# A decoder trunk on one core: the residual stream scaled once, and the MLP's operand blocks formed in a fixed order

## The chip, the cores and the metric

The kernel runs on 1 core of one Trainium2 chip. The metric is the device time of one execution in microseconds (us); lower is better. A core has TensorE (PE in the profile, with its weight loads as PEld), VectorE (DVE), ScalarE (ACT), GpSimd (POOL) and SyncE (SP), whose queue issues the DMA transfers.

## The reference, cut to what matters

One layer over 1024 tokens of width 1024: three parallel mixers behind one projection, a cross-attention to 256 memory tokens, and an MLP with a squared ReLU. The change lies in the last two sub-layers:

```
def rms_norm(x, g):
    y = x32 * lax.rsqrt(jnp.mean(x32 * x32, axis=-1, keepdims=True) + EPS)
    return y * g

h += CrossAttn(RMSNorm(h), RMSNorm(mem))        # 4 heads of 256, QK-norm, 256 memory tokens
h += W_down( relu(RMSNorm(h) @ W_up)^2 )        # 1024 -> 4096 -> 1024
```

Everything is float32. A per-token factor can be moved past a matrix product over channels, and past the squared ReLU as its square.

## The kernel before

The stream h is held transposed, channels on partitions: eight tiles `ht[0]` to `ht[7]` of 128 x 1024 (all tokens). A float32 product is made of three faster ones: each operand is split into a rounded high half (a cast on ScalarE) and the low half that remains (a subtraction on VectorE or POOL), and high x high, high x low and low x high are summed in PSUM.

*Order.* The program is traced once; a scheduler then puts each engine's instructions in order by priority and by the times that it expects, with a higher priority for what stands under `tc.high_priority()`. PE's instructions are bound: from early on each goes through `tc.keep_in_program_order`, which puts it behind the instruction of its engine that was traced just before. VectorE, ScalarE, POOL and SP are not bound here. Small side jobs wait in a list; `step()` in the loops of matmuls takes at most one due job from it, `after(n, fn)` adds one that is due n steps later, `drain()` empties it. A pool gives out tiles by tag; a tile waits until a slot of its tag is free.

*Cross-attention.* `queries(h)` projects the queries of a head (with `rx`, the tokens' RMS factor from `factors`, due after 2 steps), `attend` queues the scores, the softmax (`rd` is the reciprocal of its sum), the turns and the values. The output projection is made in two parts: `parts0` (heads 0 and 1) for all eight tiles, then `parts1` (heads 2 and 3); `project` adds each PSUM result to `ht[i]` (L1319). PSUM has two wide tiles (`pg`, 1024 columns) and four single banks (`pss`, 512 columns).

*Start of the MLP.* The second part, `parts1`, is interleaved with the forming of the MLP's operands. For a couple of tiles i = kp and kp + 4, kp = 0 to 3: `project`; store `ht[i]` to DRAM (`d_h`); form `v` = ht x gain x rbx (L1391), where `rbx` is `rx` spread over 128 partitions (a VectorE product to `hx_dg`, PE products with a matrix of ones, two ScalarE copies) at the start of this stage. The up-projection is a fast 2 x 2 block product with seven products instead of eight (Strassen's, in Winograd's form): on the token side `v` gives four halves x11, x12, x21, x22 of 512 columns, and the differences t1 to t4. Seven of these are split per couple by `slice_of` (cast L1358, subtraction L1359) into tiles `blk` that stay for the whole up-projection.

```
                dve.tensor_sub(t2, b22, t1)
                slice_of("t2", t2)
                ...
                dve.tensor_sub(t2, b21, t2)
                slice_of("t4", t2)
```

*Up-projection.* 16 pairs of weight tiles; class `Pair` loads them, forms the sums of the weight side on VectorE (`sums`, L1459 to L1463, and L1470), splits seven stationary blocks per pair (`stationary`: cast L1421, subtraction on POOL L1422) and makes seven products of 12 matmuls (`product`). The first group of products is (0,1), (0,5), (1,1), (1,5), written as (pair, product), then 6, 2, 3, 7, 4 of pair 0 and of pair 1; each later pair goes through 6, 1, 5, 7, 2, 3, 4. `result` sums the products: `p1` is a copy of product 1 (L1495), `u2` adds product 6 (L1498), `u5` adds product 5 (L1501); then come the squared ReLU and a store to `d_r`. The temporary t2 (which becomes t4) and `u2` share one tile, t3 and `u5` another, t1 and `p1` two.

*Down-projection.* Two halves of four output tiles q = 0 to 3; q < 2 lie in the wide PSUM tiles, q >= 2 in single banks. Over 32 operands, each loaded from `d_r` (`r_in`) and split (L1074, L1075) in blocks of four, runs `product(k, q, h)`: three matmuls, h being the half of the tokens. The last block goes output by output, and each half result is multiplied by the factor `f[0]` (L1589), added to the stream (`hv`, loaded from `d_h`; L1590) and stored. `f[0]` is (r / rx)^2, where r is the RMS factor of the stream before the MLP; `factor` makes it during the up-projection from the squares of the stored `d_h`.

Of the kernel before, what the change touches and what calls it, by code (L numbers as in the profile page):

```python
# [17 lines left out]
P = 128  # L18
D = 1024
# [36 lines left out]
def trunk_kernel(tc, w_io):  # L56
# [3 lines left out]
    with ctx:  # L60
# [76 lines left out]
        d_z = dram.tile([16, P, T], F32, name="d_z")  # L137
        d_cs = dram.tile([8, 32, P], F32, name="d_cs")
        d_h = dram.tile([8, P, T], F32, name="d_h")
        d_r = dram.tile([32, P, T], F32, name="d_r")  # L140
# [107 lines left out]

        def token_rstd(pool_, acc, n, scale, eps, name):
# [5 lines left out]
            return rsqrt_small(pool_, st[:, :nt], nt, scale, eps, name)  # L255

# [951 lines left out]
        with ExitStack() as sc:  # L1208
# [4 lines left out]
            def factors():  # L1213
# [3 lines left out]
                dve.tensor_mul(rx2[0], rx[0], rx[0])  # L1217

            after(2, factors)
            xg = qp.tile([P, 2], F32, name="xg")  # L1220
            dve.tensor_scalar(xg, C("xq_g", 0, 2), 1.0 / 16, None, ALU.mult)
# [32 lines left out]
            def attend(h, qT, outs, start):  # L1254
# [10 lines left out]
                def scores(t2):  # L1265
# [14 lines left out]
                    for j in range(2):  # L1280
# [32 lines left out]

            def project(parts, slot, i2, j):
# [4 lines left out]
                dve.tensor_add(hv, hv, ps)  # L1319

# [33 lines left out]

        def slice_of(name, src):
            pool_, tag = next(spares)
            t = pool_.tile([P, 2, 512], F32R, tag=tag, name="blk")
            act.copy(t[:, 0, :], src)  # L1358
            dve.tensor_sub(t[:, 1, :], src, t[:, 0, :].bitcast(F32))  # L1359
            blocks.setdefault(name, []).append(t)  # L1360

        f = []

        def factor():

            r = token_rstd(xr, sums[0], T, 1.0 / D, EPS, "hm")
            q = xr.tile([P, NT], F32, name="rq")
            dve.reciprocal(q, rx[0])
            dve.tensor_mul(q, q, r)
            dve.tensor_mul(q, q, q)  # L1370
            rb = xr.tile([P, T], F32, tag="acc", name="rb")
            dg = opa.tile([P, T], F32, tag="ol", name="f_dg")
            f.append(rb)
            after(4, lambda: spread(xr, q, T, "f", rb, dg))

        with ExitStack() as sc:
            mp = sc.enter_context(tc.tile_pool(name="up", bufs=1))

            rbx = opd.tile([P, T], F32, tag="sl", name="rbx")
            dg = opd.tile([P, T], F32, tag="sl", name="hx_dg")  # L1380
            after(0, lambda: spread(xr, rx[0], T, "hx", rbx, dg))
            for kp in range(4):
                if kp % 2 == 0:
                    slots = [wslot(w_io["w_xo"][1, kp // 2 + 2 * q]) for q in range(2)]
                vs = []
                for q in range(2):
                    i = kp + 4 * q
                    project(parts1, slots[q], i // 2, kp % 2)
                    nc.sync.dma_start(d_h[i], ht[i])
                    v = opd.tile([P, T], F32, tag="sl", name="v")  # L1390
                    dve.scalar_tensor_tensor(v, ht[i], C("g_mlp", i), rbx, ALU.mult, ALU.mult)  # L1391
                    vs.append(v)
                    lo_, hi_ = v[:, :512], v[:, 512:]
                    if q == 0:
                        slice_of("x11", lo_)
                        t1 = mp.tile([P, 512], F32, tag="p1", name="t1", bufs=2)
                        dve.tensor_sub(t1, hi_, lo_)
                        slice_of("t1", t1)
                t2 = mp.tile([P, 512], F32, tag="u2", name="t2")
                t3 = mp.tile([P, 512], F32, tag="u5", name="t3")  # L1400
                b12, (b21, b22) = vs[0][:, 512:], (vs[1][:, :512], vs[1][:, 512:])
                dve.tensor_sub(t2, b22, t1)
                slice_of("t2", t2)
                slice_of("x21", b21)
                slice_of("x22", b22)
                dve.tensor_sub(t3, b22, b12)
                slice_of("t3", t3)
                dve.tensor_sub(t2, b21, t2)
                slice_of("t4", t2)

            nstat = [0]

            def stationary(src):
# [8 lines left out]
                pool.tensor_sub(t[:, 1, :], src, t[:, 0, :].bitcast(F32))  # L1422
                return t
# [16 lines left out]
            class Pair:  # L1440
# [9 lines left out]

                def sums(self, n):

                    if n not in self.s:
                        a11, a12, a21, a22 = self.a
                        if n == 2:
                            self.sums(1)
                        self.s[n] = t = mp.tile([P, 512], F32, tag="s", name="s", bufs=3)
                        if n == 1:
                            dve.tensor_add(t, a21, a22)  # L1459
                        elif n == 2:  # L1460
                            dve.tensor_sub(t, self.s[1], a11)  # L1461
                        else:
                            dve.tensor_sub(t, a11, a21)  # L1463
                    return self.s[n]

                def weights(self, j):
                    a11, a12, a21, a22 = self.a
                    if j == 3:
                        s2 = self.sums(2)
                        dve.tensor_sub(s2, a12, s2)  # L1470
                        src = s2
                    elif j in (1, 2, 4):
                        src = {1: a11, 2: a12, 4: a22}[j]
                    else:
                        src = self.sums({5: 1, 6: 2, 7: 3}[j])
                    self.st[j] = stationary(src)

# [36 lines left out]


            ORDER = (6, 1, 5, 7, 2, 3, 4)
            groups = [[(0, 1), (0, 5), (1, 1), (1, 5)] + [(pr, j) for pr in range(2) for j in (6, 2, 3, 7, 4)]]
            groups += [[(pr, j) for j in ORDER] for pr in range(2, 16)]
            for group in groups:
                pairs = {}  # L1520
                with tc.high_priority():
                    for pr, j in group:
                        if pr not in pairs:
                            pairs[pr] = Pair(pr)
                        pairs[pr].weights(j)
                for pr, j in group:
                    if j == ORDER[0] and 2 <= pr < 10:
# [6 lines left out]
        if True:  # L1534
            for hf in range(2):
                outs = []
                for q in range(4):
                    if q < 2:
                        ps = pg.tile([P, T], F32, tag="g", name="ps_d")
                        outs.append([ps[:, :512], ps[:, 512:]])  # L1540
                    else:
                        outs.append([pss.tile([P, 512], F32, tag="s", name="ps_d2") for h in range(2)])
                hs = []
                for blk in range(8):
# [36 lines left out]
                    for q in range(4):  # L1581
                        i = hf * 4 + q
                        o = hp.tile([P, T], F32, tag=f"ht{i}", name="o")
                        for h in range(2):
                            sl = slice(h * 512, h * 512 + 512)
                            for k in range(4):
                                product(k, q, h)
                            step()
                            dve.tensor_mul(o[:, sl], outs[q][h], f[0][:, sl])  # L1589
                            dve.tensor_add(o[:, sl], o[:, sl], hs[q][:, sl])  # L1590
                            nc.sync.dma_start(w_io["outT"][i][:, sl], o[:, sl])

# [106 lines left out]
```

## Time and profile before

| what | value |
|---|---|
| three runs | 2753.6, 2754.24, 2755.34 us; median 2754.24 |
| the profiled execution | 2757.7 us, its span 2755.9 us |
| PE busy | 2701.6 us, 98% of the span |
| VectorE busy | 1635.2 us, 59% |
| ScalarE busy | 1054.2 us, 38% |
| POOL busy | 883.9 us, 32% |
| mean granted TensorE clock | 0.992 |

The span runs from the first to the last instruction. Rows of the timeline give start, duration, engine, line, operation, output <- inputs, shapes and count; in brackets stands how long the engine was idle before, and what released it. A row with "x9" merges nine instructions. Rows of waits give the engine that waited, for which engine and line, the sum in us, how often, and the longest. Rows of groups give count, busy us, mean ns, and idle time before.

### The profile page before, as it was taken

The page shows a single profiled execution, that of the slowest core. Times are in us where ns is not written, and L with a number is a line of the kernel's source. Part 1 is how long each engine was busy: PE and PEld are TensorE (multiplying, and loading weights), DVE is VectorE, ACT ScalarE, POOL GpSimd, SP SyncE. Part 2 cuts the span into 40 slices and gives each one's busy share as a digit, 9 for nine tenths or more (in the row PEclk, how much of TensorE's full clock was granted, in tenths as well). Part 3 has the DMA queues.
Part 4 walks back from the last instruction along what each step waited for, and adds up shares of the span by engine and source line. Part 5 has one row for each costly group of instructions (what it writes and reads, how often), then busy time and mean ns, then how long its engine had stood idle before and what let it go on. Part 6 is the DMA issues. An engine that isn't in the chain of part 4 may idle for free. (4 is left out here: it accounts for less than half of the span.)

```text
span 2755.9 us, 32424 instructions
## 1 busy us (share of the span) xinstructions
PE 2701.6 (98%) x12720; PEld 2183.4 (79%) x12720; DVE 1635.2 (59%) x1883; ACT 1054.2 (38%) x1780; POOL 883.9 (32%) x442
## 2 busy tenths in 40 slices
PE   9999999999999999999899999999998999999999
PEld 7888878887787878765588878899776888888787
DVE  7588878758777876634314774323367886522423
ACT  6523321123555555556511351236433322232221
POOL 2322211202625253424242432321115664322120
PEclk9999999999999999999999999999999999999999
DMA  7542232321333232442444333311123332554541
GB/s 251 196 130 99 100 107 94 107 99 39 119 119 119 96 126 104 165 149 75 135 174 160 108 107 99 100 54 39 47 84 107 145 130 107 186 181 145 191 131 68
DMA packets 113386, 330.19 MB, mean 120 GB/s; under 512 B 11329, under 2 KB 36433, under 8 KB 112849
## 3 DMA queue, kind: packets, MB, share of 16 engines
q1 hardware_dynamic: 113232, 328.12, 35.0%
q8 instruction: 100, 1.64, 0.2%
q14 instruction: 54, 0.43, 0.0%
HBM read 252.42 MB, written 78.80 MB: 120 GB/s over the span
## 5 line engine op out<-in xcount | busy, mean ns | idle before, releaser
L160 POOL TENSOR_TENSOR wl<-ws,wh 128x1024 fp32r<-128x1024 f32 (+1 forms) x153 | 383.6, 2509 | 1058.3 <-ACT wh L159 996.2
L336 DVE SCALAR_TENSOR_TENSOR tapy<-hin,cst,tapy 128x1024 f32<-128x1024 f32 x240 | 387.6, 1615 | 31.8 <-ACT tapy L331 25.5
L159 ACT CAST wh<-ws 128x1024 fp32r<-128x1024 f32 (+1 forms) x169 | 176.3, 1044 | 450.1 <-PE ps_g L73 271.4
L73 PE MATMUL ps_g<-uh,wh 128*128 128x512 f32 x1008 | 330.1, 406 | 2.0 <-ACT uh L369 1.5
L73 PE MATMUL ps_g<-ul,wh 128*128 128x512 f32 x1008 | 323.7, 396 | 0.5 <-DVE ul L370 0.5
L73 PE MATMUL ps_up<-blk,st 128*128 128x512 f32 x1344 | 311.3, 394 | 8.9 <-DVE blk L1359 5.7
L73 PE MATMUL ps_g<-uh,wl 128*128 128x512 f32 x1008 | 315.6, 392 | 1.5 <-POOL wl L160 1.5
L73 PEld LDWEIGHTS ps_up<-blk,st 128*128 128x128 f32 x1344 | 255.3, 190 | 64.2 <-DVE blk L1359 6.3
L73 PE MATMUL ps_g<-oh,wh 128*128 128x512 f32 x768 | 245.7, 401 | 6.6 <-ACT oh L1074 4.0
L73 PE MATMUL ps_g<-ol,wh 128*128 128x512 f32 x768 | 238.0, 391 | 2.7 <-DVE ol L1075 2.7
L73 PE MATMUL ps_g<-oh,wl 128*128 128x512 f32 x768 | 237.1, 390 | 0.0
L73 PEld LDWEIGHTS ps_g<-ul,wh 128*128 128x128 f32 x1008 | 189.8, 188 | 50.5 <-issue 9.3
L1075 DVE TENSOR_TENSOR ol<-r_in,oh 128x1024 fp32r<-128x1024 f32 x64 | 95.2, 1491 | 219.4 <-ACT oh L1074 219.4
L73 PEld LDWEIGHTS ps_g<-uh,wl 128*128 128x128 f32 x1008 | 190.0, 188 | 42.4 <-POOL wl L160 1.9
L73 PE MATMUL ps_d<-oh,wh 128*128 128x512 f32 x512 | 200.8, 392 | 3.1 <-DVE o L1589 3.1
L73 PE MATMUL ps_d<-ol,wh 128*128 128x512 f32 x512 | 200.8, 392 | 2.4 <-DVE ol L1075 2.1
L73 PEld LDWEIGHTS ps_g<-uh,wh 128*128 128x128 f32 x1008 | 178.4, 190 | 31.1 <-ACT uh L369 1.9
L73 PE MATMUL ps_d<-oh,wl 128*128 128x512 f32 x512 | 200.2, 391 | 0.0
L73 PEld LDWEIGHTS ps_g<-oh,wh 128*128 128x128 f32 x768 | 143.2, 188 | 42.7 <-issue 10.1
L73 PE MATMUL ps_tm<-wh,uh 128*128 128x512 f32 x448 | 175.8, 392 | 0.9 <-DVE glu_th L315 0.6
L73 PE MATMUL ps_tm<-wh,ul 128*128 128x512 f32 x448 | 174.5, 390 | 0.0
L73 PE MATMUL ps_tm<-wl,uh 128*128 128x512 f32 x448 | 174.4, 389 | 0.0
(381 smaller groups left out, 4666.8 us busy)
## 6 DMA issues: line engine op xcount, KB each, us to landing
r_in<-d_r SPq DMA_DIRECT2D x64, 512.0 KB, 3.8
ws<-w_ch SPq DMA_DIRECT2D x63, 512.0 KB, 3.6
csb<-d_cs SPq DMA_DIRECT2D x32, 512.0 KB, 3.7
gth<-d_th SPq DMA_DIRECT2D x32, 512.0 KB, 4.4
ws<-w_up SPq DMA_DIRECT2D x32, 512.0 KB, 3.3
d_r<-r SPq DMA_DIRECT2D x32, 512.0 KB, 2.6
ws<-w_down SPq DMA_DIRECT2D x32, 512.0 KB, 3.4
d_th<-gate_th SPq DMA_DIRECT2D x21, 512.0 KB, 4.9
```

Source lines behind the costliest of these rows:

```text
L73: ins = nc.tensor.matmul(*a, **k)
L159: act.copy(wh[:, a:b], st[:, a:b])
L160: (low or pool).tensor_sub(wl[:, a:b], st[:, a:b], wh[:, a:b].bitcast(F32))
L336: dve.scalar_tensor_tensor(y, hin[:, j:j + T], w(j), y, ALU.mult, ALU.add)
L1075: dve.tensor_sub(b, src, a.bitcast(F32))
```

## The change

1. The stream is scaled in place by `rx` during the queries: `scale_stream` (due after 4 steps) spreads `rx`, stores the spread to `d_rx`, and queues eight VectorE products `ht[i] x rx`. The softmax's `rd` is multiplied by `rx`, so that the attention's result is scaled alike. `v` is then ht x gain, made on ScalarE. At the end the stream is scaled back: `d_rx` is loaded during block 4 of the first half, its reciprocal taken (1024 wide), and each `hv` multiplied by it. `factor` multiplies the mean square twice by 1 / rx.
2. In the start of the MLP the VectorE and ScalarE instructions are bound in program order. The cast of a block (`slice_hi`) and its subtraction are traced apart: of a couple's seven low halves four are held back behind the next couple's first addition. The stationary blocks of pair 0 and those of (1,1) and (1,5) are made within this order, their low halves on VectorE instead of POOL.
3. In the last block of each half of the down-projection, for q < 2 the operand index k is the outer loop and the two token halves the inner one, and the result leaves 1024 wide.

```diff
+            hx = q2.tile([P, 2, T], F32, tag="xqT", name="hx")
+            def scale_stream():
+                spread(xr, rx[0], T, "hx", hx[:, 1, :], hx[:, 0, :])
+                nc.sync.dma_start(d_rx, hx[:, 1, :])
+                for i in range(KT):
+                    after(1 + i, lambda i=i: dve.tensor_mul(ht[i], ht[i], hx[:, 1, :]))
             after(2, factors)
+            after(4, scale_stream)
...
                     dve.reciprocal(rd[:, pr2], rs[:, pr2])
+                    dve.tensor_mul(rd[:, pr2], rd[:, pr2], rx[0][:, pr2])
...
-        def slice_of(name, src):
+        bound = tc.keep_in_program_order
+        def slice_hi(name, src):
             pool_, tag = next(spares)
             t = pool_.tile([P, 2, 512], F32R, tag=tag, name="blk")
-            act.copy(t[:, 0, :], src)
-            dve.tensor_sub(t[:, 1, :], src, t[:, 0, :].bitcast(F32))
+            bound(act.copy(t[:, 0, :], src))
             blocks.setdefault(name, []).append(t)
+            return lambda: bound(dve.tensor_sub(t[:, 1, :], src, t[:, 0, :].bitcast(F32)))
...
-                act.copy(t[:, 0, :], src)
-                pool.tensor_sub(t[:, 1, :], src, t[:, 0, :].bitcast(F32))
+                hi_ = act.copy(t[:, 0, :], src)
+                if early:
+                    bound(hi_)
+                    bound(dve.tensor_sub(t[:, 1, :], src, t[:, 0, :].bitcast(F32)))
+                else:
+                    pool.tensor_sub(t[:, 1, :], src, t[:, 0, :].bitcast(F32))
...
+            def take(i):
+                kp, q = i % 4, i // 4
+                if q == 0 and kp % 2 == 0:
+                    slots[:] = [wslot(w_io["w_xo"][1, kp // 2 + 2 * n]) for n in range(2)]
+                project(parts1, slots[q], i // 2, kp % 2, bound)
+                nc.sync.dma_start(d_h[i], ht[i])
+                v = opd.tile([P, T], F32, tag="sl", name="v")
+                bound(act.activation(v, ht[i], AF.Copy, scale=C("g_mlp", i)))
+                return v[:, :512], v[:, 512:]
...
+            def couple(kp):
+                b11, b12 = take(kp)
+                x11 = slice_hi("x11", b11)
+                for lo_ in late:
+                    lo_()
+                late.clear()
+                t1 = temp("p1", 2)
+                bound(dve.tensor_sub(t1, b12, b11))
+                t1_ = slice_hi("t1", t1)
+                yield
+                b21, b22 = take(kp + 4)
+                x11()
+                t1_()
+                yield
+                t2, t3 = temp("u2"), temp("u5")
+                x21, x22 = slice_hi("x21", b21), slice_hi("x22", b22)
+                bound(dve.tensor_sub(t2, b22, t1))
+                t2_ = slice_hi("t2", t2)
+                bound(dve.tensor_sub(t3, b22, b12))
+                t2_()
+                yield
+                if kp < 3:
+                    t3_ = slice_hi("t3", t3)
+                    bound(dve.tensor_sub(t2, b21, t2))
+                    late.extend([x21, x22, t3_, slice_hi("t4", t2)])
+                    return
+                x21()
+                yield
+                x22()
+                yield
+                t3_ = slice_hi("t3", t3)
+                bound(dve.tensor_sub(t2, b21, t2))
+                t3_()
+                yield
+                slice_hi("t4", t2)()
...
+            first[0].weights(1, True)
+            last = couple(3)
+            next(last)
+            first[0].weights(5, True)
+            next(last)
+            first[1].weights(1, True)
+            first[1].weights(5, True)
+            for j in (6, 2, 3, 7, 4):
+                next(last, 0)
+                first[0].weights(j, True)
...
+                        if n == 16 and not hf:
+                            f.append(opc.tile([P, T], F32, tag="oh", name="irx"))
+                            nc.sync.dma_start(f[1], d_rx)
+                            dve.reciprocal(f[1], f[1])
                         if 20 <= n < 24:
                             hs.append(opd.tile([P, T], F32, tag="sl", name="hv"))
                             nc.sync.dma_start(hs[-1], d_h[hf * 4 + n - 20])
+                            dve.tensor_mul(hs[-1], hs[-1], f[1])
...
+                        if q < 2:
+                            for k in range(4):
+                                for h in range(2):
+                                    product(k, q, h)
+                            leave(slice(0, T), wide[q])
+                            continue
```

The sums of a pair (`sums`) are bound too where they belong to an early block, and pair 0's weights are loaded after couple 1, pair 1's after couple 2, both under high priority.

More of the change, by code (lines that the diff above doesn't have):

```diff
@@ L138, in trunk_kernel @@
         d_cs = dram.tile([8, 32, P], F32, name="d_cs")
+        d_rx = dram.tile([P, T], F32, name="d_rx")
         d_h = dram.tile([8, P, T], F32, name="d_h")
@@ L247, in rsqrt_small, with token_rstd @@
             return r
-        def token_rstd(pool_, acc, n, scale, eps, name):
+        def token_rstd(pool_, acc, n, scale, eps, name, by=None):
             nt = n // P
@@ L254, in token_rstd @@
                 pe.matmul(st[:, t:t + 1], acc[:, t * P:(t + 1) * P], ones[:, 0:1], start=True, stop=True)
-            return rsqrt_small(pool_, st[:, :nt], nt, scale, eps, name)
+            st = st[:, :nt]
+            if by is not None:
+                su = pool_.tile([P, nt], F32, tag=name + "_u", name=name + "_u")
+                dve.tensor_mul(su, st, by)
+                dve.tensor_mul(su, su, by)
+                st = su
+            return rsqrt_small(pool_, st, nt, scale, eps, name)
         def spread(pool_, r, n, name, out, dg=None):
@@ L1312, in attend, with project @@
                     after(start + at, lambda fn=fn, args=args: fn(*args))
-            def project(parts, slot, i2, j):
+            def project(parts, slot, i2, j, bound=lambda ins: ins):
                 wh, wl = last_slot[0] = slot
@@ L1318, in project @@
                 hv = ht[i2 * 2 + j]
-                dve.tensor_add(hv, hv, ps)
+                bound(dve.tensor_add(hv, hv, ps))
             last_slot = [None]
@@ L1377, in trunk_kernel, with stationary @@
             mp = sc.enter_context(tc.tile_pool(name="up", bufs=1))
[L1379 to L1409, printed above, removed]
             nstat = [0]
-            def stationary(src):
+            def stationary(src, early):
                 n = nstat[0] % 10
@@ L1449, in __init__, with sums @@
                     self.s = {}
-                def sums(self, n):
+                def sums(self, n, bound):
                     if n not in self.s:
@@ L1474, in weights @@
                     else:
-                        src = self.sums({5: 1, 6: 2, 7: 3}[j])
-                    self.st[j] = stationary(src)
+                        src = self.sums({5: 1, 6: 2, 7: 3}[j], keep)
+                    self.st[j] = stationary(src, early)
                 def product(self, j):
@@ L1513, in result @@
                             nc.sync.dma_start(d_r[self.pr * 2 + r], self.r[r])
+            first = {}
+            slots = [None, None]
+            def take(i):
[7 more added lines that the diff above has]
+                return v[:, :512], v[:, 512:]
@@ new lines, in temp @@
+            def temp(tag, bufs=None):
+                return mp.tile([P, 512], F32, tag=tag, name="t", bufs=bufs)
+            late = []
+            def couple(kp):
[33 more added lines that the diff above has]
+                slice_hi("t4", t2)()
@@ new lines, in trunk_kernel @@
+            for kp in range(2):
+                for _ in couple(kp):
+                    pass
+            with tc.high_priority():
+                first[0] = Pair(0)
+            for _ in couple(2):
+                pass
+            with tc.high_priority():
+                first[1] = Pair(1)
+            first[0].weights(1, True)
[5 more added lines that the diff above has]
+            first[1].weights(5, True)
@@ L1516, in trunk_kernel @@
+            for j in (6, 2, 3, 7, 4):
+                next(last, 0)
+                first[0].weights(j, True)
+            for _ in last:
+                pass
             ORDER = (6, 1, 5, 7, 2, 3, 4)
-            groups = [[(0, 1), (0, 5), (1, 1), (1, 5)] + [(pr, j) for pr in range(2) for j in (6, 2, 3, 7, 4)]]
+            head = [(0, 1), (0, 5), (1, 1), (1, 5)]
+            groups = [[(pr, j) for pr in range(2) for j in (6, 2, 3, 7, 4)]]
             groups += [[(pr, j) for j in ORDER] for pr in range(2, 16)]
-            for group in groups:
+            for n, group in enumerate(groups):
@@ L1523, in trunk_kernel @@
                         if pr not in pairs:
-                            pairs[pr] = Pair(pr)
-                        pairs[pr].weights(j)
-                for pr, j in group:
+                            pairs[pr] = first[pr] if pr in first else Pair(pr)
+                        if pr:
+                            pairs[pr].weights(j)
+                for pr, j in (head if n == 0 else []) + group:
                     if j == ORDER[0] and 2 <= pr < 10:
@@ L1535, in trunk_kernel @@
             for hf in range(2):
-                outs = []
+                outs, wide = [], []
                 for q in range(4):
@@ L1539, in trunk_kernel @@
                         ps = pg.tile([P, T], F32, tag="g", name="ps_d")
+                        wide.append(ps)
                         outs.append([ps[:, :512], ps[:, 512:]])
```

27 lines of the change are left out of this document (14 added, 13 removed).

## The prediction

> **What bounds the kernel now.** I read the head of the page, then the list of what TensorE (PE) waited for, then stretches of the span side by side, then the timeline of each engine in the two places where PE had lost time.
>
> ```profile
> span 2755.9 us, 32424 instructions
> ...
> PE 2701.6 (98%) x12720; PEld 2183.4 (79%) x12720; DVE 1635.2 (59%) x1883; ACT 1054.2 (38%) x1780; POOL 883.9 (32%) x442
> ```
> ```profile
> PE ps_up L73 <- DVE blk L1359: 5.7, 2, 4.3
> ...
> PE ps_d L73 <- DVE o L1589: 3.1, 4, 0.8
> ...
> PE ps_d L73 <- DVE ol L1075: 2.1, 1, 2.1
> ```
> ```profile
> 2069.30:2104.66 35.36, 26.42 (x93) 20.38 (x92) 29.97 (x34) 13.70 (x24) 18.91 (x13) 0.81 0.22 75
> ```
> ```profile
> 2580.00:2720.00 140.00, 140.00 (x620) 115.95 (x619) 37.31 (x28) 36.69 (x35) 21.57 (x9) 1.00 0.41 137
> ```
>
> PE is busy for 98% of the span, so only PE time can be won: its waits, and the matmuls that run slowly after them. The waits on the list lie where the change works. The window rows (columns: stretch; length; busy time and count of PE, PEld, DVE, ACT, POOL; granted clock; DMA share; GB/s) show the start of the up-projection at a clock of 0.81, with PE busy for 26.42 of 35.36 us, and a steady stretch at 1.00. A matmul 512 wide costs 140.00/620 = 0.226 us from start to start. Now PE's timeline at the start of the up-projection:
>
> ```profile
> 2052.82 0.70 PE L73 MATMUL ps_g<-oh,wh 128*128 128x512 f32 x2 [2.62 <-DVE ht L1319]
> ...
> 2069.30 2.20 PE L73 MATMUL ps_up<-blk,st 128*128 128x512 f32 x9
> 2073.43 0.51 PE L73 MATMUL ps_up<-blk,st 128*128 128x512 f32 x1 [1.93 <-ACT blk L1358]
> 2078.28 4.36 PE L73 MATMUL ps_up<-blk,st 128*128 128x512 f32 x11 [4.35 <-DVE blk L1359]
> 2083.99 0.50 PE L73 MATMUL ps_up<-blk,st 128*128 128x512 f32 x1 [1.35 <-ACT blk L1358]
> 2085.81 4.63 PE L73 MATMUL ps_up<-blk,st 128*128 128x512 f32 x10 [1.31 <-DVE blk L1359]
> 2089.39 15.89 PE L73 MATMUL ps_up<-blk,st 128*128 128x512 f32 x64
> 2104.66 10.59 PE L73 MATMUL ps_up<-blk,st 128*128 128x512 f32 x46
> ```
>
> Counts before 2104.66: 9+1+11+1+10+64 = 96, eight products of 12. At 0.226 us these are 21.7 us; they took 2104.66 - 2069.30 = 35.4. The last projection before them ended 2.7 us late (the 2.62 us wait and a slow pair). The other place is the last block of each half of the down-projection:
>
> ```profile
> 2546.91 0.49 PE L73 MATMUL ps_d<-oh,wh 128*128 128x512 f32 x1
> 2549.50 0.80 PE L73 MATMUL ps_d<-ol,wh 128*128 128x512 f32 x1 [2.09 <-DVE ol L1075]
> 2550.09 0.63 PE L73 MATMUL ps_d<-oh,wl 128*128 128x512 f32 x1
> 2551.50 0.79 PE L73 MATMUL ps_d<-oh,wh 128*128 128x512 f32 x1 [0.78 <-DVE o L1589]
> ...
> 2573.98 0.39 PE L73 MATMUL ps_d<-oh,wh 128*128 128x512 f32 x1
> ```
> ```profile
> 2728.82 0.39 PE L73 MATMUL ps_d<-oh,wh 128*128 128x512 f32 x1
> 2729.34 0.50 PE L73 MATMUL ps_d<-ol,wh 128*128 128x512 f32 x1
> ```
> ```profile
> 2751.35 0.69 DVE L1589 TENSOR_TENSOR o<-ps_d,rb 128x512 f32<-128x512 f32 x1 [1.30 <-PE ps_d L73]
> ```
>
> A last block has 96 matmuls. The 10th (first of k = 3) starts at 2546.91 and the next half begins at 2573.98: 27.1 us for 87 matmuls that need 19.7, so 7.4 are lost: the wait for the last operand's low half, the waits for VectorE's reading (second half-tile of q = 0 and q = 1), and matmuls of 0.63 instead of 0.39 us behind them. In the second half, from the 10th at 2728.82: 86 x 0.226 + 0.39 (one matmul's length) puts the end at 2748.6, and VectorE starts on the last result at 2751.35, so 2.7 are lost.
>
> **The change part by part.** *Start of the up-projection.* Rows of VectorE, ScalarE and POOL there:
>
> ```profile
> L1391 DVE SCALAR_TENSOR_TENSOR v<-ht,cst,rbx 128x1024 f32<-128x1024 f32 x8 | 10.2, 1280 | 0.2
> L1319 DVE TENSOR_TENSOR ht<-ht,ps_g 128x1024 f32<-128x1024 f32 x7 | 8.5, 1215 | 0.7 <-PE ps_g L73 0.7
> ```
> ```profile
> 2050.87 0.68 DVE L1359 TENSOR_TENSOR blk<-t,blk 128x512 fp32r<-128x512 f32 x1
> 2051.47 1.21 DVE L1319 TENSOR_TENSOR ht<-ht,ps_g 128x1024 f32<-128x1024 f32 x1
> ...
> 2079.82 1.77 DVE L1463 TENSOR_TENSOR s<-ws 128x512 f32<-128x512 f32 x1
> ...
> 2098.53 0.69 DVE L1498 TENSOR_TENSOR u<-p,ps_up 128x512 f32<-128x512 f32 x1
> ```
> ```profile
> 2031.13 0.62 ACT L1358 CAST blk<-v 128x512 fp32r<-128x512 f32 x1 [6.19 <-DVE v L1391]
> ```
> ```profile
> 1737.76 1.15 ACT L1077 ACTIVATE oh<-ht,cst 128x1024 fp32r<-128x1024 f32 x1 [0.67 <-DVE ht L1200]
> ```
> ```profile
> 2079.32 3.42 POOL L1422 TENSOR_TENSOR st<-ws,st 128x512 fp32r<-128x512 f32 x2
> ```
>
> Half-wide VectorE operations follow each other every 0.60 us (2050.87, then 2051.47). Per couple of channel tiles VectorE now does two additions (1.2 each), two `v` (1.28 each) and eleven half-wide operations: 2.4 + 2.6 + 6.6 = 11.6 us, against 48 matmuls x 0.226 = 10.9 us on PE: VectorE falls behind, and the addition at 2051.47 comes late. After the change `v` is on ScalarE (1.15 each; with seven casts of 0.62 that is 6.6 us per couple), and VectorE needs 9.0: PE no longer waits during the projections. The last one ends at 2069.30 - 2.7 = 2066.6, the one before the last couple's second at 2061.2.
>
> From there VectorE's bound order sets the end. Between 2061.2 and the last addition stand one addition, four held-back lows, `t1`, the sum for (0,5) and its low: 1.2 + 7 x 0.60 + one cast's wait of 0.6 = 6.0, so the last addition runs 2067.2 to 2068.4. Behind it, up to `t4`'s low, are 20 bound half-wide operations (the couple's seven lows and three differences, six weight lows, four sums): 12.0, and five places where a low half waits for the cast of a value just formed, 0.6 each: 3.0. The chain ends at 2083.4. Of the stationary low halves nine move from POOL to VectorE. For collisions I take one: POOL's rows for pair 1 are ready then, and 2079.82 shows 1.77 instead of 0.68 while POOL was busy from 2079.32 on: +1.1; and one unbound sum of pair 1 put in between, 0.6: 2085.1.
>
> What is late next: `u2` of pair 0 lives in the tile that `t2`/`t4` of the last couple hold, so its addition (0.69, as at 2098.53) follows the chain's last low; only then is a PSUM bank free for product (0,3). That product starts at 2085.8, (0,7) follows, and the 97th matmul starts 24 x 0.226 = 5.4 later, at 2091.2 instead of 2104.66: **13.4 us won**. Bounds: with nothing held up but the 0.1 us that `x11`'s last low is late, 2066.6 + 0.1 + 21.7 = 2088.4, 16.3 won; with five collisions, 2095.6, 9.1 won. Early weights need slots: those of (1,1) and (1,5) come free with the slot that ends at 2061.2, the five of pair 0 with the last projection, all before their place in the chain.
>
> *Last blocks.* With k outside and both halves inside for q = 0, the last operand is needed after 18 matmuls instead of 9, 2.0 us later; it came 2.4 us late in the first half (2549.50 against 2547.14) and 0.3 late in the second. Left: 0.4 and none. A wide result reads a tile that nothing writes afterwards, so the four waits go. The wide product and addition (about 1.2 each, like L1319) end before the next tile's, 2.7 us later, and the very last result keeps its form. **7.4 - 0.4 + 2.7 = 9.7 won.** Bounds: 4.3 (four times 0.78 and its slow matmul of about 0.3) to 10.1.
>
> *What is added or moved.* Rows for it:
>
> ```profile
> 2022.44 1.88 PE L73 MATMUL ps_bs<-hx_dg,mat 128*128 128x512 f32 x4
> ```
> ```profile
> 1842.39 0.16 DVE L1241 TENSOR_TENSOR xss<-xss,rx 128x4 f32<-128x4 f32 x1 [13.97 <-ACT xjunk L1239]
> ```
> ```profile
> L659 DVE RECIPROCAL dt_a<-dt_a 128x256 f32<-128x256 f32 x1 | 1.8, 1752 | 0.0
> ```
> ```profile
> 2437.32 1.23 DVE L1075 TENSOR_TENSOR ol<-r_in,oh 128x1024 fp32r<-128x1024 f32 x1 [4.21 <-ACT oh L1074]
> ```
> ```profile
> PE ps_bs L73 <- DVE f_dg L262: 0.2, 1, 0.2
> ```
>
> The spread of the factors (four PE passes, two copies, one 1.2 us VectorE product) moves from 2022 into the queries: nothing on PE. There VectorE stands idle for 13.97 us after the factors exist, which covers the product; the eight scalings of 1.2 fall into gaps of the queries' normalisation; the store on SP has nothing urgent behind it. If that cover is gone, a turn of queries waits: 0 to 2 us, I take 0. Sixteen tiny products (0.16) in the attention: 0, two on the way to `f_dg`: 0.4, since PE already waits for it. In the down-projection a reciprocal 1024 wide, an estimate of four times the 1752 ns at 256: 7.0 us; eight products of 1.2; one load. VectorE idles 4.21 of each 5.4 us there and runs three operands ahead (16 us), so 0; if the reciprocal floats to the start of the down-projection, up to 3; below nothing I see no way. **Sum: 13.4 + 9.7 - 0.4 = 22.7.**
>
> **The rivals.** *Port.* The bound lows collide with POOL's work for pair 1 every time. The rows: 0.68 without, 1.77 with POOL running. Five collisions instead of one put the 97th matmul at 2095.6: 18.4 won, 2735.8. [...] *Results behind the bound row.* If ScalarE's copy of pair 0's first product stands behind the bound casts (2083), product (0,6) starts there: four products later it is 2094.5, plus 3 us of matmuls at 0.63: 7.2 won there, 2737.7. The unbound copies in between at present speak against it. *Operand late again.* If ScalarE puts one more weight cast (1.05) and POOL's collision ahead of the last operand, the first half keeps some 4 of its 7.4, an estimate from the 2.09 us wait and the slow matmuls behind it: 19.1 won, 2735.1. *VectorE as the bound* (the other sign): per couple PE waits for 11m + 2.4 - 10.9, m being a half-wide operation's mean. The whole gain is gone at m = 1.29, slower by over 0.2% from 1.41; at m = 1.6 the time is 2768. For it: 1.77 us operations; against: they come with POOL, which by the code has four weight splits in that stage.
>
> **How the numbers follow.** The profiled execution took 2757.7 us, its span 2755.9; the median shown, 2754.24, lies 3.5 below. The gain goes off the median: 2754.24 - 22.7 = 2731.5. Chances: forecast (2728 to 2735) 0.54; port 0.18; results behind 0.09; operand late 0.10; VectorE the bound within 0.2% of before 0.04, slower 0.05. Low end 2727: the upper bounds 16.3 + 10.1, and 1 us more. High end 2744: the rivals that still win, two of them together. 0.2% is about what a measurement here tells from no change. Faster 0.91, same 0.04, slower 0.05.
>
> **What will show it.** PE without a wait for `ht` in the projections; the first up products behind one another at clock 1.00 with one wait of a few us before (0,3), released by `u2`; no wait for `o` in the last blocks; irx's reciprocal near 7 us with PE undisturbed. Wrong if VectorE's chain after the last addition is far from 15 us, or if a new wait stands in the queries.

## The result, and the profile after

The forecast was 2731.5 us, a gain of 22.7. The changed kernel took 2760.44 us (median of 20 runs, 2751.05 to 2763.98) beside 2755.01 for the kernel before on the same chip (20 runs): ratio 1.0020, 95% interval 1.0014 to 1.0026. It is slower by 0.2%. The profiled execution took 2761.03 us, its span 3.4 us longer than that of the kernel before (whose profiled execution, 2757.7 us, lies in the upper part of its runs; hence 5.4 by the medians). Head of the page of the changed kernel:

```profile
span 2759.2 us, 32441 instructions
...
PE 2704.0 (98%) x12720; PEld 2186.1 (79%) x12720; DVE 1659.2 (60%) x1911; ACT 1062.1 (38%) x1788; POOL 863.3 (31%) x433
```

PE is still busy for 98%, so the waits of PE come next (engine waited for; us, times, longest):

```profile
PE ps_up L73 <- ACT st L1410: 7.0, 1, 7.0
...
PE ps_d L73 <- DVE ol L1083: 5.3, 2, 5.1
...
PE ps_d L73 <- DVE r L1504: 3.6, 1, 3.6
...
PE ps_up L73 <- DVE blk L1382: 2.3, 1, 2.3
...
PE ps_up L73 <- DVE r L1504: 2.0, 1, 2.0
```

The old rows (`blk` 5.7, `o` 3.1, `ol` 2.1, and `ht` 2.62 in the timeline) are gone, and five new ones add up to 20.2 us. Two of them stand in `ps_d`, where the prediction saw no cost. The same as a table by stage, windows of the changed kernel (columns as in the prediction): projections of `parts1`; first 96 products' matmuls; first and last block of the first half of the down-projection; the same of the second half.

```profile
2021.04:2064.58 43.54, 43.54 (x194) 36.06 (x192) 32.51 (x43) 23.20 (x32) 4.81 (x2) 1.00 0.34 132
2064.58:2100.46 35.88, 24.63 (x97) 19.20 (x96) 30.53 (x39) 15.10 (x26) 12.76 (x9) 0.90 0.22 74
2392.05:2420.42 28.37, 24.72 (x98) 19.85 (x96) 20.36 (x15) 7.24 (x7) 8.79 (x4) 0.88 0.81 304
2551.01:2573.27 22.26, 22.04 (x97) 17.91 (x96) 13.77 (x11) 4.88 (x5) 5.58 (x3) 1.00 0.64 211
2573.27:2602.44 29.17, 24.08 (x97) 19.44 (x96) 15.67 (x13) 7.21 (x8) 4.12 (x2) 0.88 0.56 199
2733.01:2754.77 21.76, 21.76 (x97) 17.84 (x95) 10.28 (x11) 1.05 (x1) 0.00 (x0) 1.00 0.20 77
```

And of the kernel before: projections, first 96 matmuls, the first block of each half.

```profile
2021.06:2069.30 48.24, 45.62 (x198) 36.72 (x196) 39.83 (x48) 16.36 (x27) 11.85 (x6) 1.00 0.32 119
2069.30:2105.57 36.27, 27.33 (x97) 21.13 (x96) 29.97 (x34) 13.70 (x24) 19.82 (x13) 0.81 0.22 77
2392.48:2414.27 21.79, 21.79 (x97) 17.94 (x96) 10.58 (x10) 8.45 (x9) 6.17 (x3) 1.00 0.81 299
2573.98:2596.21 22.23, 22.09 (x97) 17.94 (x96) 10.88 (x9) 7.22 (x8) 4.83 (x2) 1.00 0.68 241
```

The ledger, after minus before, from these rows and the starts of PE's matmuls:

| stretch | before | after | difference |
|---|---|---|---|
| ahead of the projections of `parts1` | 2021.06 | 2021.04 | 0.0 |
| projections of `parts1` | 48.24 | 43.54 | -4.7 |
| first 96 matmuls of the up-projection | 36.27 | 35.88 | -0.4 |
| next 72 (to the end of pair 1) | 16.32 | 18.23 | +1.9 |
| pairs 2 to 15 | 270.6 | 273.4 | +2.8 |
| down-projection, two first blocks | 21.8 + 22.2 | 28.4 + 29.2 | +13.5 |
| down-projection, two last blocks | 29.15 + 24.37 | 22.29 + 21.76 | -9.5 |
| behind the last matmul | 4.7 | 4.5 | -0.2 |

Sum +3.4, the difference of the spans. What the last blocks won, the first blocks lost and more. Two rows need care. The first holds two things that cancel: in this execution the changed kernel reached the queries 1.7 us sooner (1810.70 against 1812.41; the stages ahead of them are the same code), and it then spent 1.7 us more in them. Of the +1.9, 1.6 us are nine matmuls at half pace (0.43 us each instead of 0.227), which two kernels below with the same code in this stage do not have (the reciprocal alone kept in place, and 128 bytes: 16.6 us for the 72). The chain that ended last has the two steps by name (start, us, step):

```profile
2392.90 6.46 DVE irx L1636
...
2567.38 6.17 DMA hv<-d_h
```

VectorE and then PE at both places:

```profile
2392.82 6.55 DVE L1636 RECIPROCAL irx<-irx 128x1024 f32<-128x1024 f32 x1
2399.28 1.22 DVE L1504 TENSOR_TENSOR r<-u,ps_up 128x512 f32<-128x512 f32 x2
...
2573.58 1.23 DVE L1640 TENSOR_TENSOR hv<-hv,irx 128x1024 f32<-128x1024 f32 x1 [2.13 <-DMA hv<-d_h]
2574.72 2.84 DVE L1669 TENSOR_TENSOR o<-o,hv 128x512 f32<-128x512 f32 x1
2577.48 1.21 DVE L1083 TENSOR_TENSOR ol<-r_in,oh 128x1024 fp32r<-128x1024 f32 x1
```
```profile
2399.96 0.79 PE L73 MATMUL ps_d<-oh,wh 128*128 128x512 f32 x1 [3.65 <-DVE r L1504]
...
2578.75 0.79 PE L73 MATMUL ps_d<-ol,wh 128*128 128x512 f32 x1 [5.09 <-DVE ol L1083]
```

In the first half the scheduler has put the reciprocal, whose products the results first read some 165 us later (at 2558.39), ahead of the last results of pair 15, whose PSUM bank PE needs at once. In the second, a product `hv` that waits for its load stands ahead of the first operands' low halves. PE waits 3.65 us in the first and 5.09 us in the second, and both times then runs at 0.43 us a matmul for a while. Now the start of the up-projection, PE, then VectorE, then POOL:

```profile
2064.58 2.43 PE L73 MATMUL ps_up<-blk,st 128*128 128x512 f32 x10
2069.33 14.44 PE L73 MATMUL ps_up<-blk,st 128*128 128x512 f32 x62 [2.32 <-DVE blk L1382]
2090.71 7.77 PE L73 MATMUL ps_up<-blk,st 128*128 128x512 f32 x24 [6.95 <-ACT st L1410]
2100.46 5.74 PE L73 MATMUL ps_up<-blk,st 128*128 128x512 f32 x17 [1.98 <-DVE r L1504]
```
```profile
2085.95 0.68 DVE L1382 TENSOR_TENSOR blk<-t,blk 128x512 fp32r<-128x512 f32 x1
2086.55 1.75 DVE L1413 TENSOR_TENSOR st<-ws,st 128x512 fp32r<-128x512 f32 x1
2088.22 1.75 DVE L1464 TENSOR_TENSOR s<-ws,s 128x512 f32<-128x512 f32 x1
2089.89 0.68 DVE L1492 TENSOR_TENSOR u<-p,ps_up 128x512 f32<-128x512 f32 x1
...
2092.46 1.76 DVE L1452 TENSOR_TENSOR s<-ws 128x512 f32<-128x512 f32 x1
...
2097.96 1.76 DVE L1464 TENSOR_TENSOR s<-ws,s 128x512 f32<-128x512 f32 x1 [1.45 <-POOL st L1415]
2099.64 0.68 DVE L1504 TENSOR_TENSOR r<-u,ps_up 128x512 f32<-128x512 f32 x1
```
```profile
2086.39 3.03 POOL L1415 TENSOR_TENSOR st<-s,st 128x512 fp32r<-128x512 f32 x2 [7.83 <-ACT st L1410]
```

The wait of 6.95 us is put down to a cast, but PE's matmul at 2090.71 follows the end of `u2` (2089.89 + 0.68), which frees the PSUM bank. `t4`'s low half is done at 2086.63; then come a bound low half and a free sum of pair 1, 1.75 us each while POOL runs, and only then `u2`. The wait of 1.98 is of the same kind: `r` behind pair 2's free sums.

Pairs 2 to 15 have no wait that is new, and yet are 0.19 us longer each. Eight pairs, 672 matmuls, before and after:

```profile
2140.93:2293.25 152.32, 152.32 (x674) 126.13 (x672) 118.77 (x121) 45.11 (x70) 92.80 (x63) 1.00 0.35 132
```
```profile
2137.91:2291.73 153.82, 153.82 (x674) 126.27 (x672) 119.04 (x121) 45.09 (x71) 92.86 (x63) 1.00 0.36 130
```

PE is busy throughout at a granted clock of 1.00, with the same work on every engine; its matmuls are slower. By their starts, averaged over six pairs, those that read the four `blk` tiles in pool `opd` and up to some six behind them take up to 236 ns, all others 226 to 228. What differs for these tiles is their address. The new small tile `hm_u` (32 bytes a partition) in a pool ahead of them moves `opd`, in the compiled program, from address 189632 to 189664. In the kernel before, every tile that PE streams there starts at 192 modulo 256. (The pool `up` behind `opd` moves with it, but PE reads nothing from `up`.)

### The profile page after: what moved, and what is told of

Same layout as the page of the kernel before. It is cut to its first block, busy times and chain, and to the rows that moved or that the text cites. A ratio compares the mean times of both kernels' runs of the same rounds, so it can differ in the third digit from the quotient of the medians.

```text
span 2759.2 us, 32441 instructions
## 1 busy us (share of the span) xinstructions
PE 2704.0 (98%) x12720; PEld 2186.1 (79%) x12720; DVE 1659.2 (60%) x1911; ACT 1062.1 (38%) x1788; POOL 863.3 (31%) x433
```

## Experiments: the down-projection

**Both floating operations kept in their place** (the changed kernel with):

```
-  dve.reciprocal(f[1], f[1])
+  bound(dve.reciprocal(f[1], f[1]))
...
-  dve.tensor_mul(hs[-1], hs[-1], f[1])
+  bound(dve.tensor_mul(hs[-1], hs[-1], f[1]))
```

> The changed kernel with the reciprocal of the spread factors and the eight products that scale the stream back bound in program order, so that each stands on VectorE behind the operand split traced before it. Theory (VectorE's queue in the first block of each half holds back results and operands): the first blocks fall from 28.4 and 29.2 us to about 21.8 and 22.2, 13.5 us in all, time near 2747. Rival (the added loads on the DMA queue hold the operands up, not the queue of VectorE): the loads are the same, the first blocks stay above 26 us, time near 2760.

Measured: 2747.6 us, ratio 0.9976 (0.9966 to 0.9986), 12 us under the changed kernel by the two ratios. The first blocks take 21.78 and 22.19 us, as before the change. What is left of PE's waits there, and the reciprocal's new place:

```profile
PE ps_d L73 <- DVE ol L1083: 0.2, 1, 0.2
```
```profile
L1636 DVE RECIPROCAL irx<-irx x1: 6539/6539/6539, 2462.4 to 2462.4; 128x1024 f32<-128x1024 f32 x1
```

The same 6.54 us cost nothing at 2462.4. It was their place that cost; the loads are the same, so the rival falls.

**The reciprocal alone kept in place.**

> The changed kernel with only the down-projection's reciprocal kept in program order; the hv products still free. Theory (two separate stalls, one for each half): the first half's first block 21.8 us instead of 28.4, the second half's stays at 29.2; 6.6 us won, ratio about 0.9998 (2754). Rival (the hv products' early place follows from the reciprocal's): both first blocks 21.8 to 22.2, ratio about 0.9976.

Measured: 2752.39 us, ratio 0.9992 (0.9983 to 1.0001). First half's first block 21.78 us, second half's 29.87. Two stalls, then, one in each half; in the second the same rows as before:

```profile
2564.54 1.23 DVE L1640 TENSOR_TENSOR hv<-hv,irx 128x1024 f32<-128x1024 f32 x1 [2.08 <-DMA hv<-d_h]
...
2568.44 1.21 DVE L1083 TENSOR_TENSOR ol<-r_in,oh 128x1024 fp32r<-128x1024 f32 x1
```

**The last blocks' order alone**, put into the kernel before (all k inside q, wide results read once; the scaling as it was; `leave` multiplies by the factor, adds `hv` and stores):

```
+  if q < 2:
+      for k in range(4):
+          for h in range(2):
+              product(k, q, h)
+      leave(slice(0, T), wide[q])
+      continue
```

> The kernel before with the last block of each half alone changed: k outside and the token halves inside for q < 2, and a wide result. Theory (the last blocks gave what the trace shows, 6.9 and 2.6 us): time near 2745.5, last blocks 22.3 and 21.8 us instead of 29.2 and 24.4. Rival (the gain is given back in the first block of the second half whatever is done there): last blocks shorter, first block of the second half longer, time near 2752 to 2755.

Measured: 2744.95 us, ratio 0.9966 (0.9952 to 0.998); last blocks 22.27 and 21.76 us, halves 174.63 and 174.52. The waits for `o` and all but 0.2 us for `ol` are gone:

```profile
PE ps_d L73 <- DVE ol L1075: 0.2, 1, 0.2
```

By itself this part of the change is worth 9.4 us by the ratio (5.5 to 13.2 by its interval) and 9.5 in the trace, where the prediction gave it 9.7.

## Experiments: the slower matmuls

**The kernel before, with an unused tile of 32 bytes** ahead of `opd`, and nothing else of the change:

```
+  gap = xr.tile([P, NT], F32, name="gap")
+  pool.memset(gap, 0.0)
```

> The kernel before with one unused tile of 32 bytes per partition (set to zero once by POOL) in the pool of the factors, nothing else changed. Theory (the shift alone slows the matmuls): 19.2 instead of 19.04 us a pair, 2.7 to 3 us more over 16 pairs, time near 2758. Rival: 19.04 and 2755.

Measured: 2758.23 us, ratio 1.0014 (1.0005 to 1.0023). Eight pairs:

```profile
2140.33:2294.14 153.81, 153.81 (x673) 126.17 (x672) 117.45 (x121) 45.18 (x70) 92.66 (x63) 1.00 0.36 130
```

An unused tile makes the kernel before slower, by the same 0.19 us a pair as the change. Three kernels widen the changed kernel's `su` so that `opd` lies 64, 128 and 256 bytes above its old place (the diff of the first; `4 * nt` and `8 * nt` in the others):

```
-  su = pool_.tile([P, nt], F32, tag=name + "_u", ...)
+  su = pool_.tile([P, 2 * nt], F32, tag=name + "_u", ...)[:, :nt]
```

64 bytes:

> The changed kernel with the small tile of the factor's sums padded from 32 to 64 bytes per partition, so that the pool behind it starts at the same multiple of 64 bytes as in the kernel before. Theory (32 bytes of shift make the matmuls slow whose operand blocks lie in that pool): a pair of the up-projection takes 19.04 instead of 19.23 us, 2.7 us in all, time near 2757.8. Rival (the slow matmuls come from the new order of the blocks or from other engines' work): 19.23 stays, time near 2760.4.

Measured: 2757.95 us, ratio 1.0015 (1.0006 to 1.0024). The time is near the forecast, but the theory is not confirmed: the pairs are no faster.

```profile
2138.88:2293.17 154.29, 154.29 (x673) 126.12 (x672) 117.59 (x121) 45.10 (x70) 93.65 (x63) 1.00 0.35 130
```

128 bytes:

> The changed kernel with su 128 bytes wide instead of 32, so that the four tiles of pool opd (moving operands of the up-projection) and all of pool up start 128 bytes, instead of 32, above their place in the kernel before; nothing else changed. In the kernel before, every tile that TensorE reads as a moving operand there starts at an address that is 64 modulo 128 and 192 modulo 256; shifts of 32 and of 64 bytes both gave pairs of 19.23 to 19.29 us instead of 19.04. Theory A (the start's residue modulo 128 decides): pairs 19.04 us and matmuls on opd at 227 ns as before, the time 2.5 to 4 us under the changed kernel, ratio about 1.0005. Theory B (modulo 256 or more): pairs 19.2 to 19.3, ratio about 1.002 as without the padding. Theory C (the shift moved some other thing, not the phase): also 19.2 to 19.3, and then in the combined kernel of this set, with 256 bytes, too.

Measured: 2758.5 us, ratio 1.0018 (1.0009 to 1.0026); pairs of 19.20 us, theory B or C:

```profile
2136.52:2290.12 153.60, 153.60 (x673) 126.14 (x672) 117.47 (x121) 45.08 (x70) 93.19 (x63) 1.00 0.35 131
```

256 bytes, together with the edits at the other two places (below: the combined kernel):

```profile
2137.54:2289.86 152.32, 152.32 (x674) 126.17 (x673) 117.32 (x121) 45.16 (x70) 93.10 (x63) 1.00 0.36 132
```

The old pace is back. Shifts of 32, 64 and 128 bytes are slow, 0 and 256 are not. That fits a pace set by the tile's start modulo 256; the point of 256 bytes was taken only in kernels with other edits as well. Whether the slow part is the start address itself or that it differs from that of the other streamed tiles (all at 192 modulo 256) stays open; no run moved all of them.

## Experiments: the start of the up-projection

**The temporaries exchanged**, so that `u2` no longer needs the tile of `t4`:

```
-  t2, t3 = temp("u2"), temp("u5")
+  t2, t3 = temp("u5"), temp("u2")
```

> The changed kernel with the two temporaries of the couples exchanged: t2/t4 in the tile of u5, t3 in that of u2, so that pair 0's u2 no longer waits for t4's low half, only for t3's. Theory (the gate on u2's tile holds product (0,3) back): the addition u2 runs about 6 us sooner, before pair 1's sums; (0,3) starts near 2084 instead of 2090.7 with at most a short wait, no half-rate products behind it, the 97th matmul at about 2092 instead of 2100.5; 6 to 9 us won against the changed kernel, about 2752, ratio 0.999. Rival (VectorE's row with pair 1's sums and POOL's collisions is the limit): the wait only moves, to (0,7) and (0,4), which need u5 and r, and under 3 us are won, ratio 1.0015 to 1.002.

Measured: 2757.76 us, ratio 1.0013 (1.0004 to 1.0022). Product (0,3) starts at 2084.33 as the theory has it, but (0,7) then waits longer than ever:

```profile
2084.33 3.00 PE L73 MATMUL ps_up<-blk,st 128*128 128x512 f32 x12 [1.68 <-DVE u L1492]
2090.86 12.88 PE L73 MATMUL ps_up<-blk,st 128*128 128x512 f32 x48 [3.52 <-DVE r L1504]
```

The 97th matmul starts 31.8 us after the projections instead of 35.9, and the first 168 take 51.9 instead of 54.1. By the two ratios it is 2 us faster than the changed kernel, as the rival says. The gate on `u2`'s tile was real, and so was the rival: behind the gate stands the next addition, itself behind pair 1's sums. **The combined kernel**: both bound operations, the exchange, the shift of 256 bytes.

> The changed kernel with four edits: the reciprocal and the hv products of the down-projection kept in program order, the temporaries exchanged, and su 256 bytes wide (tiles of opd at the same residue modulo 256 as in the kernel before). If the effects add: 12.8 (down-projection) + 6 to 9 (start of the up-projection) + 2.5 to 4 (matmul rate) under the changed kernel's 2760.4, that is 2735 to 2739, ratio 0.993 to 0.9945, and pairs of 19.04 us. If the phase of the tiles is not the cause of the slow matmuls: pairs 19.2 to 19.3 and 2738 to 2742. If the exchange gives nothing: 2743 to 2746.

Measured: 2744.78 us, ratio 0.9965 (0.9952 to 0.9977). That misses the sum of the effects and lies in the range given for an exchange that gives nothing: the first 168 matmuls take 53.4 us here, with waits of 2.30, 1.76, 3.51 and 2.50. Of the 1.5 us more than with the exchange alone, nine half-pace matmuls behind the wait of 2.30 are 1.6.

**Free temporaries**: `t2` to `t4` in a tile that no result uses, and `x11`'s last low half ahead of the last projection's addition (with the combined kernel's other edits; the exchange falls away):

```
+  w23 = xr.tile([P, T], F32, tag="acc", name="t23")
+  t2, t3 = w23[:, :512], w23[:, 512:]
...
+  if kp == 3:
+      x11()
   yield
   b21, b22 = take(kp + 4)
-  x11()
+  if kp < 3:
+      x11()
```

> The kernel with all four edits, and two more at the start of the up-projection: t2/t3/t4 of every couple in a tile that no result uses (tag acc of pool xr), so that u2 and u5 of pair 0 wait for no temporary, and the low half of the last couple's x11 formed before its second projection's addition instead of behind it. Theory (tile gate and x11's place are what is left): product (0,5) follows (0,1) without the 2.3 us wait, (0,3) starts without a wait, the first 168 products' matmuls take 44 to 48 us instead of 53.4, the time is 2736 to 2740, ratio about 0.994. Rival (pair 1's sums and POOL's collisions on VectorE hold the results back whatever tile they use): still waits of 2 to 4 us before (0,3), (0,7) or pair 1's products, 50 us or more, 2741 or more, ratio about 0.9955.

Measured: 2741.18 us, ratio 0.9955 (0.9942 to 0.9969). The wait of 2.3 us is gone, and (0,3) follows without one. (0,7) waits for a result behind pair 1's sum, which itself waits for POOL:

```profile
2089.16 16.74 PE L73 MATMUL ps_up<-blk,st 128*128 128x512 f32 x60 [5.88 <-DVE r L1504]
```
```profile
2086.08 1.73 DVE L1464 TENSOR_TENSOR s<-ws,s 128x512 f32<-128x512 f32 x1 [1.16 <-POOL st L1415]
```

51.0 us for the 168: between theory and rival, the rival's wait. **Pair 1's sums bound** behind pair 0's chain, `bound(dve.tensor_sub(...))` traced after it:

> As the kernel with the free temporaries, and pair 1's sums kept in program order behind pair 0's chain of low halves instead of floating in ahead of it (their low halves stay on POOL). Theory (the floating sums, slowed to 1.75 us by POOL, are what holds the results back): all eight products of pair 0's head and (0,3), (0,7), (0,4) run with no wait over 1 us, the first 168 matmuls take 40 to 43 us instead of 53.4, the time is 2731 to 2735, ratio 0.992. Rival (pair 1's products then come late by as much as pair 0's gain): waits of 2 us and more move to (1,6) to (1,4), 46 to 50 us, as the kernel with the free temporaries or slower, 2738 to 2742.

Measured: 2741.06 us, ratio 0.9956 (0.9944 to 0.9969). Pair 0 now runs as the theory has it: the 97th matmul starts 25.0 us after the projections, 0.4 more than the prediction's 24.6. The 168 still take 50.7 us, for pair 1 waits. The first wait is put down to a cast, but the matmul follows `u` (2092.60), which stood behind a free sum of pair 2 at 1.77 us; the second follows an addition behind another:

```profile
2093.42 4.29 PE L73 MATMUL ps_up<-blk,st 128*128 128x512 f32 x12 [2.05 <-ACT st L1410]
...
2103.89 12.34 PE L73 MATMUL ps_up<-blk,st 128*128 128x512 f32 x45 [2.82 <-DVE r L1517]
```

**Pair 1's additions bound too**, pair 2's sums behind them:

```
+  keep = bound if self.pr == 1 or self.pr == 0 and j in (7, 4) else lambda ins: ins
-  dve.tensor_add(self.u2, self.p1, banks[6])
+  keep(dve.tensor_add(self.u2, self.p1, banks[6]))          (and the other additions)
+  if (pr, j) == (1, 2):
+      for j2 in ORDER:
+          first[2].sums_of(j2)
```

> As the kernel with pair 1's sums bound, and pair 2's sums bound behind pair 1's second product, with the additions that free PSUM banks (pair 0's last three, all of pair 1) bound ahead of them. In the kernel before this one, PE's waits before pair 1's products (2.05, 0.23 and 2.82 us, and the half-rate matmuls behind them) ended with additions that stood on VectorE behind pair 2's sums at 1.7 us each. Theory: those waits go, the first 168 matmuls take 41 to 46 us instead of 50.7, 2732 to 2737, ratio 0.993 to 0.994. Rival (POOL's low halves of 1.3 to 1.7 us each, of which pair 1's last and pair 2's follow one another, are then what is late): waits of the same sum before pair 1's last products or pair 2's first, 49 us or more, or a first pair behind them of over 21 us; 2739 to 2743.

Measured: 2740.0 us, ratio 0.9946 (0.9932 to 0.9959), the fastest, though its interval overlaps those of the two before it. The first 168 matmuls and pair 2:

```profile
2063.31:2106.25 42.94, 40.86 (x170) 30.60 (x168) 36.22 (x50) 17.06 (x30) 14.83 (x10) 1.00 0.25 88
2106.25:2130.52 24.27, 21.06 (x85) 16.91 (x86) 22.40 (x22) 7.88 (x12) 16.47 (x12) 0.93 0.49 170
```

42.9 us as the theory has it (38.1 without any wait), and 5.2 us lost again in pair 2, behind pair 3's sums. **The same for pairs 2 to 4:**

> As the kernel with pair 1's additions bound, the same now for pairs 2 to 4: their additions bound, the sums of pairs 3 to 5 bound behind the third product of the pair before. In the kernel before this one PE waited 3.21 us (and ran half-rate behind it) in pair 2 for an addition that stood behind pair 3's sum and a square of 1.74 to 1.77 us each. Theory (the floating sums are still the cause): pair 2 takes 19.04 to 20 us instead of 24.3, no later pair over 20 (but for the one with the factor, 23.06), 2734 to 2737, ratio 0.993. Rival (VectorE and POOL are behind with the work itself, whatever its order): the same 4 to 5 us appear in pair 2 or spread over pairs 2 to 5, 2739 to 2742.

Measured: 2744.94 us, ratio 0.9963 (0.9951 to 0.9975). The median is 4.9 us above that of the kernel before it and beyond the rival's range, though the two intervals overlap slightly. Pairs 2 to 5 take 21.4, 24.8, 19.3 and 21.8 us, 87.3 in all against 81.4 there. A bound sum overwrites a tile that POOL still reads, and the bound addition behind it waits with it:

```profile
2148.14 1.73 DVE L1463 TENSOR_TENSOR s<-ws,s 128x512 f32<-128x512 f32 x1 [3.66 <-POOL st L1415]
```
```profile
2150.52 26.55 PE L73 MATMUL ps_up<-blk,st 128*128 128x512 f32 x108 [3.91 <-DVE u L1511]
```

Whether another order would remove this loss, or VectorE and POOL together have too much to do here, stays open: in the fastest kernel VectorE was busy for 22.40 of pair 2's 24.27 us (the window row from 2106.25), many of its operations at 1.75 us beside POOL, while in this one it stood idle for POOL.

## Why the prediction was wrong, step by step

The forecast was a gain of 22.7 us, the result a loss of 5.4. Of the 28 us between, the down-projection's added work is 13.5, the start of the up-projection about 12, and the shifted tiles nearly 3.

*The step that failed first: the down-projection's added work at 0.* Reciprocal and products were costed by what VectorE has free in the middle of the stage (4.21 of each 5.4 us), with 3 us as the bound "if the reciprocal floats to the start". It did float there, and the bound was the wrong one: it measured 6.55 us (7.0 forecast) and 6.6 us of PE's time, since the addition that frees pair 15's bank stood behind it. That the `hv` products could do the same in the second half, waiting for a load, was not thought of: 6.9 us more. The binding runs show both: 13.5 us of the ledger, where the sum had 0. (In the other kernels with the same free operations the two first blocks took 27.3 to 28.4 and 25.8 to 29.9 us.)

*The start of the up-projection: 13.4 became 3.2* (4.7 + 0.4 - 1.9 in the ledger), and 1.5 when the 1.7 us that moved into the queries are counted. The projections run without the wait, as forecast. Some 1.7 of their 4.7 us is the spread of `rx`, whose four matmuls now stand in the queries. The forecast called that move free, but its 2066.6 for the end of the projections still held the spread; PE began the up-projection at 2064.58. The chain from the last addition to `t4`'s low half took 19.2 us (2067.46 to 2086.63) where 17.9 were forecast, so that part was sized well, and the gate of `u2` on `t4`'s tile was there. Mis-sized was the rest: PE waited 2.3 us for `x11`'s low half instead of 0.1, mostly because it came 2.0 us sooner itself; a weights' low half and a free sum stood between the chain and `u2`, 3.3 us; and the forecast did not have the half-pace matmuls behind the waits, nor the next wait, for `r`. In the kernel with the sums bound these are gone, and the eight products take the forecast time; the loss then appears one pair later. So the cause is the row of VectorE as a whole: free sums of the next pair ahead of additions that free a bank. (The prediction also took 2104.66 for the start of the 97th matmul before; it is 2105.57, four matmuls later.)

*A term that was missing: 2.8 us* for the shift of `opd` by a 32-byte tile (2.6 over the same pairs in the kernel before with the unused tile). The tiny products were costed, the tile that they need was not.

*Right:* the last blocks (9.7 forecast, 9.5 in the ledger, 9.4 by the ratio of that part alone). The factor's 0.4 us do not show: its pair takes 23.24 us against 23.07, no more than the shift's 0.19. The queries cost 1.7 us more (131.1 against 129.4, from their first matmul to the first output projection). That is within the 0 to 2 given, but not for the reason given, a turn that waits: it is nearly all the spread's four matmuls, and the projections of `parts1` win it back.

*The rivals:* the collisions with POOL came: VectorE's 512-wide additions and subtractions with both inputs in SBUF that started while POOL ran took 1.17 to 1.80 us, most of them 1.75, against 0.68. But that rival put the 97th matmul at 2095.6; it started at 2100.46, because additions that free a bank stood behind the slowed rows, and half-pace matmuls followed PE's waits. No rival had the down-projection, which alone turns the sign: with its two operations bound the change takes 2747.6 us, ratio 0.9976, instead of 2760.44; with the shift mended and the temporaries exchanged as well, 2744.78.

## What to carry to other kernels

Work added to an engine that is mostly idle is free only if the order leaves it behind what PE waits for (here a reciprocal of 6.5 us cost PE 6.6 us in one place and nothing in another): ask of every operation that a scheduler may move what it could be put in front of, and bind the one with slack rather than the ones in need. Binding more is not better: in a bound row each instruction inherits the wait of the one before it (with pairs 2 to 4 bound, a sum waited 3.66 us for POOL, and PE 3.91 us for the addition behind that sum). And read the compiled addresses after any change of tiles: a shift of 32 bytes cost 2.6 to 2.8 us here.

## What the runs showed of the hardware that was not expected

- PE's pace went with where a streamed tile starts: 19.20 to 19.29 us per 84 matmuls with four of 28 tiles shifted by 32, 64 or 128 bytes, 19.04 with 0 or 256, at a granted clock of 1.00 in all.
- A wait of PE can cost more than itself: in the changed kernel ten matmuls behind 6.95 us took 4.4 us instead of 2.3 (0.43 us each against 0.227; the granted clock was 0.50 in 2090.71:2094.55, 1.00 in 2069.33:2083.77). Behind short waits it differed from run to run of the same code: behind 1.98 us four ran at full pace and then nine took 3.65 us instead of 2.04 (granted clock 0.50 in 2101.86:2105.27), but with the reciprocal alone kept in place none was slow behind nearly the same wait (1.93 us). Behind the 2.32 us before the 11th matmul none was slow, but in the kernel with 128 bytes eight took 3.41 us (wait 2.31) and in the combined kernel nine took 3.65 (wait 2.30).
- RECIPROCAL at 128x1024 took 6.55 us, a little under four times the 1.75 us at 128x256.
